# A 1024x6400 input projection: seven block products instead of eight for 34 of 50 column tiles on half of the tokens

## The chip, the cores and the metric

The kernel runs on one core of a Trainium2 chip. The core has a matrix engine (TensorE, PE in the profile, with its weight loads as PEld), a vector engine (VectorE, DVE), an engine for functions (ScalarE, ACT), a general one (GpSimd, POOL) and SyncE (SP), whose queue issues most of the DMAs here. The engines run at the same time and wait for each other by semaphores; each takes its own instructions strictly in the order of the program. The metric is the device time in microseconds, lower is better.

## What is computed

One layer of a decoder: a wide projection of 2080 tokens (2048 of a prompt, 32 of a sample group), three branches that mix tokens, a gate for each, an output projection and a layer norm.

```python
proj = x @ p['w_in']                      # (2080 x 1024) @ (1024 x 6400)
q, k, v, g_a, u_b, g_b, x_c, g_c, g_m = jnp.split(proj, _split_points(), axis=-1)
attn = _attn_prompt(q, k, v, ...)         # sliding window of 128, 8 heads
y_b = _s5_branch(u_b, ...)                # complex state-space scan, then a GLU
y_c = _rglru_branch(x_c, ...)             # convolution of 4, gated linear recurrence
ya = (attn * silu(g_a)) @ p['w_br_a']     # yb, yc in the same way from y_b, g_b and y_c, g_c
merged = sigmoid(g_m)[a] * ya + sigmoid(g_m)[b] * yb + sigmoid(g_m)[c] * yc
y = layernorm(DN_ALPHA * x + merged @ p['w_out'])
```

## The kernel before

Everything is float32. A product of two float32 matrices is made as three matmuls (`mm3`, L98 to L101): each operand is split into a high part (ACT, line L89) and the rest (DVE, L94 or L96), and high x high, high x rest and rest x high are added up in PSUM.

**Main line.** The 6400 columns of `w_in` are 50 tiles of 128 columns (`TILES`, 0 to 49, in the order u, x, k, v, q: 14 tiles; m: 24 tiles; gc, gb, ga: 4 each). The tokens are 5 units (`UN`): units 0, 1 and 2 of 512 tokens, units 3 and 4 of 272. Units 0 and 1 are called the first 1024 tokens here, units 2 to 4 the later ones. X, transposed and split, stays in SBUF (`xh0` to `xh4`, `xl0` to `xl4`). For a tile and a unit, `gemm` runs 8 blocks of the contraction x 3 matmuls into one of three PSUM banks (tag `mm`), and `evac` takes it out: a q, k, v, x or m tile by one ACT instruction and a store; a gate tile (gc, gb, ga) by ACT (tanh), DVE (L104, tanh+1 times the value) and DVE (L233, or L225 for gb, times the branch's result, loaded by `gate_load`), and a store of the product (`actD`). The weights of the next tile are split once in a tile (`w_split`, 128x1024 on ACT and DVE) and those after it are loaded (`w_load`).

**Side streams.** Four generators do the branches one after the other: `s5_stream`, `glu_stream`, `lru_stream`, `attn_stream`. The order on every engine is written out by hand: after each block of `gemm`, `tick(n)` adds 3n/2400 us to a counter, and when this has reached the value that the stream yielded last (`STEP` 4.6 where it gave none; 2.5 and 3.5 in turn for attention), the stream's next piece is emitted, its matmuls between those of the main line. So the side work of a microsecond of projection is fixed by these values, not by how far the engines are. The attention has 32 full steps (two for each of 16 blocks of 128 tokens). The gate tiles need the branch's result: gc that of the LRU (`hD`), gb that of the GLU (`zD`), ga that of the attention (`aD`).

**After the projection** come the branch projections (`y_unit`, tag `py`), where the last ga tile overlaps with the loads and splits of their operands (`seam`), and the output projection with the layer norm (`out_mm`, `out_ln`).

## Time and profile before

| | us |
|---|---|
| time, median of 3 runs | 1802.98 (1802.05 to 1808.93) |
| the profiled execution's own time | 1802.31 |
| its span, first to last instruction | 1800.6 |

The profile lists, for each engine, when its instructions began and ended. Matmuls are pipelined: one is listed longer than the time until the next begins, so the distance of starts is what one costs, and a share of busy time of PE near 100% tells little. For DVE, ACT and POOL a busy time is a real occupation of the engine. A line number is that of the kernel before; a helper (L89, L94, L96, L104) stands for many places, which the tile names tell apart. Side work and main line lie in the same stretches, so each stage is read by its own window.

### The profile page before, as it was taken

How to read it: one execution, taken by the hardware profiler on the slowest of the kernel's cores; microseconds unless marked ns; L12 is line 12 of the kernel's file. 1: busy time of each engine (PE TensorE's matmuls, PEld its weight loads, DVE VectorE, ACT ScalarE, POOL GpSimd, SP SyncE). 2: the span in 40 equal slices, each digit the busy share in tenths (PEclk: the TensorE clock that was granted, in tenths of full speed). 3: DMA queues.
4: the chain of work that ended last, by engine and by line, in shares of the span. 5: the costliest groups of instructions: out<-in, count | busy, mean ns of one | idle time of the engine just before them, and what ended most of it. 6: DMA issues, size and time to landing. Idle time of an engine off the chain costs nothing. (4 is left out here: it accounts for less than half of the span.)

```text
span 1800.6 us, 26639 instructions
## 1 busy us (share of the span) xinstructions
PE 1777.6 (99%) x9788; PEld 1548.2 (86%) x9788; DVE 1130.1 (63%) x2450; ACT 654.4 (36%) x1382; POOL 167.9 (9%) x377
## 2 busy tenths in 40 slices
PE   8999999999999999999999999999999999999998
PEld 7888888888899888888988888888888888888886
DVE  5755888885334455653777899644343657666666
ACT  6312443343333377674656555311221212120110
POOL 0000000000000000000355555400000000000000
PEclk9999999999999999999999999999999999999999
DMA  7443433442333334443332344453454646542222
GB/s 234 111 135 100 114 105 110 116 115 87 119 118 114 101 99 117 113 98 90 108 108 80 119 123 127 126 148 106 145 180 147 190 141 197 163 133 94 94 94 76
DMA packets 214039, 220.36 MB, mean 122 GB/s; under 512 B 89125, under 2 KB 156709, under 8 KB 212741
## 3 DMA queue, kind: packets, MB, share of 16 engines
q1 hardware_dynamic: 182532, 169.27, 33.3%
q10 hardware_dynamic: 31376, 49.39, 7.6%
q8 instruction: 77, 1.26, 0.3%
q14 instruction: 54, 0.43, 0.1%
HBM read 136.53 MB, written 83.14 MB: 122 GB/s over the span
## 5 line engine op out<-in xcount | busy, mean ns | idle before, releaser
L99 PE MATMUL mm<-xh,wh 128*128 128x512 f32 (+1 forms) x1920 | 678.3, 353 | 0.0
L101 PE MATMUL mm<-xh,wl 128*128 128x512 f32 (+1 forms) x1920 | 672.9, 350 | 0.0
L100 PE MATMUL mm<-xl,wh 128*128 128x512 f32 (+1 forms) x1920 | 670.8, 349 | 0.0
L101 PEld LDWEIGHTS mm<-xh,wl 128*128 128x128 f32 x1920 | 360.8, 188 | 47.2 <-DVE wl L94 0.3
L99 PEld LDWEIGHTS mm<-xh,wh 128*128 128x128 f32 x1920 | 361.3, 188 | 43.6
L100 PEld LDWEIGHTS mm<-xl,wh 128*128 128x128 f32 x1920 | 361.5, 188 | 42.7
L99 PE MATMUL py<-ah,wbh 128*128 128x512 f32 (+1 forms) x480 | 169.0, 352 | 1.3 <-DVE acc L104 1.3
L101 PE MATMUL py<-ah,wbl 128*128 128x512 f32 (+1 forms) x480 | 168.9, 352 | 0.0
L100 PE MATMUL py<-ah,wbh 128*128 128x512 f32 (+1 forms) x480 | 168.8, 352 | 0.0
L89 ACT ACTIVATE st<-mm 128x512 f32<-128x512 f32 (+1 forms) x170 | 86.8, 511 | 157.0 <-PE mm L101 144.9
L99 PEld LDWEIGHTS py<-ah,wbh 128*128 128x128 f32 x480 | 90.2, 188 | 14.5 <-issue 1.7
L100 PEld LDWEIGHTS py<-ah,wbh 128*128 128x128 f32 x480 | 90.3, 188 | 12.8
L101 PEld LDWEIGHTS py<-ah,wbl 128*128 128x128 f32 x480 | 90.2, 188 | 12.5
L1492 PE MATMUL po<-wol,mh 128*128 128x512 f32 x224 | 88.8, 396 | 0.0
L1491 PE MATMUL po<-woh,mh 128*128 128x512 f32 x224 | 88.8, 396 | 0.0
L1493 PE MATMUL po<-woh,ml 128*128 128x512 f32 x224 | 88.8, 396 | 0.0
L94 DVE TENSOR_TENSOR wl<-wr,wh 128x1024 fp32r<-128x1024 f32 x48 | 58.9, 1227 | 38.4 <-ACT wh L89 38.3
L104 DVE SCALAR_TENSOR_TENSOR gt<-gt,mm 128x512 f32<-128x512 f32 (+1 forms) x60 | 35.0, 583 | 70.8 <-ACT gt L89 70.5
L104 DVE SCALAR_TENSOR_TENSOR br<-br,py 128x512 f32<-128x512 f32 (+1 forms) x80 | 46.8, 586 | 51.5 <-PE py L101 43.8
L89 ACT ACTIVATE gt<-mm 128x512 f32<-128x512 f32 (+1 forms) x60 | 30.9, 515 | 115.6 <-PE mm L101 115.6
L89 ACT ACTIVATE wbh<-wbr 128x512 fp32r<-128x512 f32 x24 | 15.1, 629 | 149.1 <-PE py L100 127.6
L89 ACT ACTIVATE wh<-wr 128x1024 fp32r<-128x1024 f32 x48 | 50.5, 1052 | 24.6 <-DMA wr<-in_w_in_dram 15.3
(347 smaller groups left out, 2736.5 us busy)
## 6 DMA issues: line engine op xcount, KB each, us to landing
wr<-in_w_in_dram SPq DMA_DIRECT2D x48, 512.0 KB
mD<-st ACTq DMA_DIRECT2D x72, 256.0 KB
br<-mD SPq DMA_DIRECT2D x71, 256.0 KB
lx<-in_xr_dram SPq DMA_DIRECT2D x16, 512.0 KB
mD<-st ACTq DMA_DIRECT2D x48, 136.0 KB
br<-mD SPq DMA_DIRECT2D x47, 136.0 KB
xr<-in_xT_dram SPq DMA_DIRECT2D x24, 256.0 KB
wbr<-in_w_br_dram SPq DMA_DIRECT2D x24, 256.0 KB
```

What stands on the lines that cost most here:

```text
L89: return A.activation(out, in_, func, bias=bias, scale=scale, **kw)
L94: V.tensor_sub(lo, src, hi)
L99: PE.matmul(ps, wh, xh, start=start, stop=False)
L100: PE.matmul(ps, wh, xl, start=False, stop=False)
L101: PE.matmul(ps, wl, xh, start=False, stop=stop)
L104: return (eng or V).scalar_tensor_tensor(out, a, s, b, op0=op0, op1=op1)
L1491: PE.matmul(ps[c], h[:, k, :rows], wh, start=k == 0, stop=False)
L1492: PE.matmul(ps[c], h[:, k, :rows], wl, start=False, stop=False)
L1493: PE.matmul(ps[c], l[:, k, :rows], wh, start=False, stop=k == 7)
```

## The change

The order of the tiles is new: 14 tiles as before on all tokens (`FULL`), then the other 36 on the later tokens only (`LATER`: ga, gb, m, gc), then two gc tiles (48, 49) on the first 1024 tokens (`fill`), and then tiles 14 to 47 on the first 1024 tokens, in 17 pairs: two gc, four gb, 22 m, four ga and two more m tiles.

A pair is a product of a 2x2 block matrix of weights (two tiles x two halves of the contraction) with a 2x2 block matrix of X (two halves of the contraction x units 0 and 1). It is computed by seven block products of 4 blocks x 3 matmuls x 512 columns in place of eight. For that, sums of X blocks are made once (`x_sums` on DVE and POOL from a fresh load of X into the room of units 3 and 4, `x_parts` splits them), and for each pair sums of weight blocks (four POOL instructions in `operand`), seven splits of 128x512, four copies out of PSUM on ACT (`keep`) and four additions with PSUM on DVE. The weights of tiles 14 to 47 are loaded a second time (`pair_load`).

The gates: a later-token gate of ga or gb is stored without its branch (`gD`), and a new stream behind the attention, `gating_stream`, loads it and the branch and multiplies on POOL. gc on the later tokens and in `fill` is gated at once as before. In a pair, `finish` gates ga, gb and gc by two DVE instructions and one on ACT.

The GLU yields 2.8 in place of 4.6 in 16 places; the transposes of v go to the PSUM bank `sc`; `act_split`, `wo_split` and `m_split` use other rooms of the same pools (`xh1` is in two halves now). The core of the diff:

```diff
...
-GLU_WEIGHTS = 2.0
+GLU_WEIGHTS, GLU = 2.0, 2.8
...
          + [("q", i) for i in range(4)]
-         + [("m", i) for i in range(24)]
-         + [("gc", i) for i in range(4)] + [("gb", i) for i in range(4)] + [("ga", i) for i in range(4)])
+         + [("gc", 0), ("gc", 1)] + [("gb", i) for i in range(4)]
+         + [("m", i) for i in range(16, 24)] + [("m", i) for i in range(8, 16)] + [("m", i) for i in range(6)]
+         + [("ga", i) for i in range(4)] + [("m", 6), ("m", 7), ("gc", 2), ("gc", 3)])
+
+
+FULL, WIN = 14, 48
+
+LATER = sorted(range(FULL, len(TILES)), key=lambda i: ("ga", "gb", "m", "gc").index(TILES[i][0]))
 IN_NAMES = ["xT", "xr", "w_in", "w_br", "w_out", "w_glu", "lru_w", "lru_v", "lru0", "conv0",
             "s5p", "s5b", "s5c", "s5cd", "s5h", "s5hx", "s5d", "relT", "sinks", "ckT", "ck", "cv", "lnp"]
...
+        elif kind == "gc":
+            br = gate_br.pop((i, u))
+            st = stage.tile([128, 512], FT, name=uid("st"), tag="st")[:, :n]
+            act(st, ps[:, :n], AF.Tanh, scale=0.5)
+            V.tensor_mul(br, ps[:, :n], br)
+            stt(st, st, 1.0, br, OP.add, OP.mult)
+            gate_st.append((actD["c"][i][:, t0:t0 + n], st))
         else:
...
+            act(st, ps[:, :n], AF.Tanh, scale=0.5)
+            stt(st, st, 1.0, ps[:, :n], OP.add, OP.mult)
+            gate_st.append((gD[kind[1]][i][:, t0:t0 + n], st))
...
-            yield
+            yield GLU
...
-            ps = psum.tile([128, 512], FT, name=uid("mm"), tag="mm", bufs=3)
+            ps = sc()
...
+    def gating_stream():
...
+        for j, (b, i) in enumerate(jobs):
+            z, g = got.pop(j)
+            if b == "b":
+                gv = g[:, 0:1024].rearrange("p (c j) -> p c j", j=8)
+                G.tensor_mul(gv, gv, z[:, :, 0:128].rearrange("p j c -> p c j"))
+                gv = g[:, 1024:1056].rearrange("p (b t) -> p b t", t=4)
+                G.tensor_mul(gv, gv, z[:, 0:4, 128:136].rearrange("p t b -> p b t"))
+            else:
+                G.tensor_mul(g, g, z)
+            LD.dma_start(actD[b][i][:, 1024:T], g)
+            load(j + 2)
+            yield
+        es.close()
...
+    units = ([(o, u) for o in range(2, len(TILES)) for u in (range(5) if o < FULL else range(2, 5))][:-3]
+             + [(len(TILES) - 1, u) for u in (3, 4, 2)])
+    fill = [(WIN, 0), (WIN, 1), (WIN + 1, 1), (WIN + 1, 0)]
+    gated = [(ORDER[o], u) for o, u in units if TILES[ORDER[o]][0] == "gc"] + fill
...
+            sides += [glu_stream(), lru_stream(), attn_stream(), gating_stream()]
...
+        if (i, u) == gated[0]:
             while not gp:
                 side_step()
...
+    r12, r11, r22, r21 = (place(x, FT) for x in ("xl3", "xh3", "xh4", "xl4"))
+    for k in range(4):
+        for r, k0, c0 in ((r12, 0, 512), (r11, 0, 0), (r22, 4, 512), (r21, 4, 0)):
+            LD.dma_start(r[:, k], I["xT"][(k0 + k) * 128:(k0 + k) * 128 + 128, c0:c0 + 512])
+
+    def x_sums(k):
+        V.tensor_sub(r11[:, k], r12[:, k], r11[:, k])
+        G.tensor_sub(r12[:, k], r22[:, k], r12[:, k])
+        V.tensor_sub(r22[:, k], r22[:, k], r11[:, k])
+        G.tensor_sub(r21[:, k], r21[:, k], r22[:, k])
...
+    for n, (i, u) in enumerate(fill):
+        gates_out()
+        gate_next((i, u))
+        ps = gemm(i, u)
+        evac(*TILES[i], u, ps)
+        tick(512)
+        if n == 1:
+            for k in range(4):
+                x_sums(k)
+        if n > 1:
+            t = place(("xl2", "xh2")[n - 2])
+            TT[4 - n] = x_parts(t[:, 0:4], t[:, 4:8], (r22, r11)[n - 2])
...
+    def pair_load(i):
...
+            for j in range(2):
+                WD.dma_start(r[:, j], I["w_in"][i + j])
...
+    def operand(q):
...
+        a11, a12, a21, a22 = r[:, 0, 0:4], r[:, 0, 4:8], r[:, 1, 0:4], r[:, 1, 4:8]
+        if j == 0:
+            s1 = wpool.tile([128, 4, 128], FT, name=uid("s1"), tag="wr", bufs=1)
+            OPS["s1"] = s1
+            G.tensor_add(s1, a21, a22)
+        src = (a11, a12, a11, OPS["s1"], a21, a12, a22)[j]
+        w = wpool.tile([128, 2, 4, 128], FR, name=uid("ws"), tag=("wh", "wl")[q % 2])
+        split(w[:, 0], w[:, 1], src)
+        if j == 0:
+            G.tensor_sub(a21, a11, a21)
+            G.tensor_sub(a11, OPS["s1"], a11)
+        if j == 1:
+            G.tensor_sub(a12, a12, a11)
...
+    def keep(ps):
+        s = spare()
+        act(s, ps, AF.Copy)
+        return s
...
+    def finish(i, u, s):
+        kind, ti = TILES[i]
+        t0, n = UN[u]
+        if kind == "m":
+            act(s, s, AF.Tanh, scale=0.5)
+            ST.dma_start(mD[ti][:, t0:t0 + n], s)
+        else:
+            z = ZS.pop((i, u))
+            v = s.rearrange("p (c j) -> p c j", j=8) if kind == "gb" else s
+            V.tensor_mul(z, v, z)
+            act(s, s, AF.Tanh, scale=0.5)
+            stt(v, v, 1.0, z, OP.add, OP.mult)
+            gate_st.append((actD[kind[1]][ti][:, t0:t0 + n], s))
...
+    AHEAD = 3
+    pair_load(FULL)
+    for q in range(AHEAD):
+        operand(q)
+    TT[3] = x_parts(place("xh3"), place("xh4"), r12)
+    TT[4] = x_parts(place("xl3"), place("xl1a"), r21)
+    pair_load(FULL + 2)
+    blk = lambda u, k0: tuple([t[k0 + k] for k in range(4)] for t in X[u])
+    parts = lambda x: tuple([t[:, k] for k in range(4)] for t in TT[x])
+    MOV = [blk(0, 0), blk(0, 4), parts(2), parts(1), parts(3), blk(1, 4), parts(4)]
+    for p in range(FULL, WIN, 2):
+        if p == WIN - 4:
+            while sides:
...
+        while TILES[p][0] == "ga" and not prompt_done[0]:
+            side_step()
+        bank, kept = {}, {}
+        for j in range(7):
+            q = (p - FULL) // 2 * 7 + j
+            w, (mh, ml) = OPS.pop(q), MOV[j]
+            into, first = ((0, True), (1, True), (0, False), (2, True), (0, False), (2, False), (3, True))[j]
+            if first:
+                bank[into] = psum.tile([128, 512], FT, name=uid("mm"), tag="mm", bufs=3)
+            ps = bank[into]
+            for k in range(4):
+                for n, (a, b) in enumerate(((w[:, 0, k], mh[k]), (w[:, 0, k], ml[k]), (w[:, 1, k], mh[k]))):
+                    PE.matmul(ps, a, b, start=first and k == 0 and n == 0, stop=k == 3 and n == 2, skip_group_check=True)
+                if k < 3:
+                    tick(512)
+            operand(q + AHEAD)
+            gates_out()
+            if j == 0 and TILES[p][0] != "m":
+                z_load(p, 0)
+                z_load(p + 1, 1)
+            if j == 3:
+                pair_load(p + 4)
+            if j == 0:
+                kept[1] = keep(ps)
+            elif j == 1:
+                V.tensor_add(kept[1], ps, kept[1])
+                finish(p, 0, kept[1])
+            elif j == 2:
+                kept[2] = keep(ps)
+            elif j == 3:
+                kept[5] = keep(ps)
+            elif j == 4:
+                V.tensor_add(kept[5], ps, kept[5])
+                kept[3] = keep(ps)
+                finish(p + 1, 1, kept[5])
+            elif j == 5:
+                V.tensor_add(kept[2], ps, kept[2])
+                finish(p, 1, kept[2])
+            else:
+                V.tensor_add(kept[3], ps, kept[3])
+                finish(p + 1, 0, kept[3])
+            seam(p, j)
+            tick(512)
...
+        if t % 4 < 2:
+            if t % 4 == 0:
+                M_["mg"] = xhp.tile([128, 2, 2, 8, 128], FR, name=uid("mg"), tag="xh2")
...
+            m = xhp.tile([128, 2, 8, 128], FR, name=uid("mo"), tag=f"xh{t % 4 + 1}")
+            h, l = m[:, 0], m[:, 1]
...
```

## Rows read from the trace of the kernel before

**Rows 1.** The page, part 1: busy time, share of the span and count by engine.
```profile
PE 1777.6 (99%) x9788; PEld 1548.2 (86%) x9788; DVE 1130.1 (63%) x2450; ACT 654.4 (36%) x1382; POOL 167.9 (9%) x377
```

**Rows 2.** Timeline of PE: start, us, engine, line, tiles, shape.
```profile
1289.64 0.39 PE L99 MATMUL mm<-xh,wh 128*128 128x512 f32 x1
...
1299.16 0.28 PE L99 MATMUL mm<-xh,wh 128*128 128x272 f32 x1
...
1303.95 0.29 PE L101 MATMUL mm<-xh,wl 128*128 128x272 f32 x1
```

**Rows 3.** Windows: stretch, its us, busy (count) PE, PEld, DVE, ACT, POOL, clock, DMA.
```profile
853.00:1150.00 297.00, 290.69 (x1764) 258.65 (x1765) 246.44 (x535) 171.86 (x535) 154.53 (x300) 1.00 0.36 110
1050.00:1100.00 50.00, 47.66 (x296) 42.34 (x295) 46.34 (x99) 26.64 (x89) 26.44 (x51) 1.00 0.44 134
300.00:400.00 100.00, 100.00 (x574) 88.67 (x573) 83.94 (x230) 41.79 (x88) 1.18 (x12) 1.00 0.39 107
```

**Rows 4.** Timeline of DVE: the first and the last scores of the attention, a gate.
```profile
854.79 0.29 DVE L1038 TENSOR_TENSOR S<-sa,B 128x128 f32<-128x128 f32 x1
...
1140.20 1.44 DVE L225 TENSOR_TENSOR st<-gt,br 128x512 f32<-128x512 f32 x1
1141.57 0.94 DVE L1040 TENSOR_TENSOR S<-sa,B 128x768 f32<-128x768 f32 x1
```

**Rows 5.** Groups of DVE in 853:1150: line, tiles, shape, count | busy, mean ns.
```profile
L94 DVE TENSOR_TENSOR wl<-wr,wh 128x1024 fp32r<-128x1024 f32 x10 | 12.4, 1244 | 2.9 <-ACT wh L89 2.9
L104 DVE SCALAR_TENSOR_TENSOR gt<-gt,mm 128x512 f32<-128x512 f32 x14 | 9.5, 680 | 0.6 <-ACT gt L89 0.5
L233 DVE TENSOR_TENSOR st<-gt,br 128x512 f32<-128x512 f32 x12 | 9.3, 777 | 0.4
L233 DVE TENSOR_TENSOR st<-gt,br 128x272 f32<-128x272 f32 x8 | 3.6, 447 | 0.3
L104 DVE SCALAR_TENSOR_TENSOR gt<-gt,mm 128x272 f32<-128x272 f32 x8 | 3.4, 428 | 0.1
L225 DVE TENSOR_TENSOR st<-gt,br 128x512 f32<-128x512 f32 x2 | 2.5, 1238 | 0.1
```

**Rows 6.** Groups of PE, whole span: the attention's matmuls.
```profile
L1026 PE MATMUL sa<-kl,q 128*128 128x192 f32 x120 | 28.4, 274 | 0.0
L1052 PE MATMUL sc<-ident,S 128*128 128x128 f32 x128 | 19.8, 278 | 3.5 <-DVE S L1012 2.7 <-ACT oo L89 0.7
L1100 PE MATMUL sb<-pth,vn 128*128 128x256 f32 x62 | 18.1, 292 | 0.7 <-POOL pth L1082 0.7
```

**Rows 7.** Groups of DVE, whole span: a split and an addition with PSUM.
```profile
L94 DVE TENSOR_TENSOR wbl<-wbr,wbh 128x512 fp32r<-128x512 f32 x24 | 16.4, 684 | 0.0
L1059 DVE TENSOR_TENSOR ptl<-sc,pth 128x512 fp32r<-128x512 f32 x32 | 21.9, 683 | 0.9 <-ACT pth L89 0.5
```

**Rows 8.** Groups of ACT, whole span: a copy out of PSUM, a split.
```profile
L89 ACT ACTIVATE st<-mm 128x512 f32<-128x512 f32 x102 | 60.2, 590 | 104.7 <-PE mm L101 102.9 <-DMA ur<-uD 1.1 <-ACT st L89 0.4
L89 ACT ACTIVATE wbh<-wbr 128x512 fp32r<-128x512 f32 x24 | 15.1, 629 | 149.1 <-PE py L100 127.6 <-DMA wbr<-in_w_br_dram 12.3 <-DVE acc L1459 9.2
```

**Rows 9.** Groups of POOL, whole span: the longest of either kind.
```profile
L1082 POOL TENSOR_SCALAR_AFFINE_SELECT pth<-pth 64x256 fp32r<-64x256 f32 x60 | 32.5, 561 | 2.0
L991 POOL CAST vn<-vn 64x512 fp32r<-64x512 f32 x16 | 12.9, 806 | 56.3 <-DVE vn L94 55.5
```

**Rows 10.** Timelines of DVE and POOL: the same DVE instruction without and beside POOL.
```profile
867.03 0.42 DVE L978 TENSOR_TENSOR kl<-kr,k 64x256 fp32r<-64x256 f32 x1
...
902.80 0.49 POOL L1082 TENSOR_SCALAR_AFFINE_SELECT ptq<-pth 64x256 fp32r<-64x256 f32 x1
...
903.05 0.51 DVE L978 TENSOR_TENSOR kl<-kr,k 64x256 fp32r<-64x256 f32 x1
```

**Rows 11.** Timelines of PE, ACT and DVE: end of one GLU product to the next.
```profile
522.12 0.40 PE L99 MATMUL mm<-xh,wh 128*128 128x512 f32 x1
...
522.32 0.61 ACT L89 ACTIVATE zs<-sb 128x528 f32<-128x528 f32 x1 [2.59 <-PE sb L101]
...
525.99 1.26 DVE L96 SCALAR_TENSOR_TENSOR zl<-zy,zh 128x1056 fp32r<-128x1056 f32 x1 [1.15 <-ACT zh L89]
...
527.59 0.28 PE L99 MATMUL sa<-zh,gluh 128*128 128x264 f32 x1
```

**Rows 12.** The page, part 2: what the DMA engines moved, 40 slices.
```profile
GB/s 234 111 135 100 114 105 110 116 115 87 119 118 114 101 99 117 113 98 90 108 108 80 119 123 127 126 148 106 145 180 147 190 141 197 163 133 94 94 94 76
```

279 lines of the change are left out of this document (163 added, 116 removed).

## The prediction

> **What bounds the kernel now.** I read the page by engine first, then the distance of matmul starts, then each stage by its window. PE is busy for 99% of the span [rows 1], which alone proves little; but the distances do: in an undisturbed unit 42 starts of 512 columns lie (1299.16 - 1289.64) / 42 = 0.2267 us apart and 38 of 272 columns (1303.95 - 1299.16) / 38 = 0.126 us [rows 2]. That is columns + 32 at 2.4 GHz, the higher clock level, in both; I use it for shapes that I don't show. A column tile then costs 24 x (3 x 0.2267 + 2 x 0.126) = 22.4 us on all tokens, and the projection's 50 tiles 1119 us of the 1800.6. So PE's matmuls are the path, and a matmul taken away is worth 0.2267 us, as long as no other engine becomes the path. The second thing to read is therefore DVE by stage: 63% over the span, but 246.4 of 297 us while the attention runs, and 46.34 of 50 where gates and attention meet; there PE is busy for 47.66 of 50 only [rows 1, 3].
>
> **What is removed.** A pair of tiles takes 7 x 4 x 3 = 84 matmuls of 512 columns instead of 96. 17 pairs x 12 x 0.2267 = 46.2 us of PE, on the path. All other matmuls stay, in number and size. The profiled execution took 1802.31 us, 0.7 under the median of 1802.98, so the sum is made against 1802.3: with nothing else, 1756.
>
> **The attention beside the pairs.** Its pieces are tied to the projection's columns, so I count them in the program. A step of the attention takes 2.5 + 3.5 of the counter; with 512 columns a block that is 4 + 6 blocks, 10 x 3 x 0.2267 = 6.8 us of projection (7.2 in the smaller units; 6.9 over the old stretch). The same count, made for the old order, puts the end of the attention into the first gb tiles; the trace has the gate of gb (L225) just ahead of the last scores [rows 4], so the count holds. From first to last scores are 31 steps in 286.8 us [rows 4], 9.25 us each: 6.9 of projection and, by counts of [rows 6], 8 x 0.093 + 4 x 0.067 + 6 x 0.12 = 1.7 of its own matmuls, with the transposes of v 1.8. The rest, 0.5 us a step or 16 us in 32 steps, PE waits already now.
>
> DVE in this stretch: 246.4 us less splits and gates, 12.4 + 9.5 + 9.3 + 3.6 + 3.4 + 2.5 = 40.7 [rows 3, 5], leaves 206 for 32 steps, 6.4 each.
>
> In the new order the count puts the first step into the second gc tile on later tokens. There follow 2.7 such tiles, the four units of `fill`, and nine pairs: gc, two gb, six m. PE needs 2.7 x 24 x (0.2267 + 2 x 0.126) = 31 us, 4 x 5.44 = 22, 9.1 x 84 x 0.2267 = 173, and 32 x 1.8 = 58: 284 us. DVE needs, from [rows 5, 7]:
> - attention: 206;
> - 2.7 later gc tiles: 1.24 + 0.68 + 0.78 + 2 x (0.43 + 0.45) = 4.5 each: 12;
> - `fill` and the sums of X: 8 sums and 16 splits at 0.68, 4 gates at 1.46: 22;
> - nine pairs: 7 splits + 4 additions = 11 x 0.68 = 7.5 each: 67;
> - their gates: gc 4 x 1.46 = 6; two gb pairs, both instructions on strided data like L225, 4 x 2 x 1.24 = 10 each: 20.
>
> That is 333 us of DVE against 284 of PE: in this stretch DVE becomes the path. The additions out of PSUM don't wait long either: a bank that held the copy's source (`keep`) is written again one product, 12 x 0.2267 = 2.7 us, later, and ACT and DVE take attention and pairs in one queue, where a unit before had two further banks. Were DVE busy all the time, the stretch is 333 us; at the share of the fullest window, 46.34 / 50 = 0.93 [rows 3], 358. I take the middle, 345. So PE waits 61 us where it waited 16: **+45, between +33 and +58**. ACT stays under it: 172 us now [rows 3], and a pair brings 7 x 0.63 + 8 x 0.59 = 9.1 us [rows 8], nine of them 82.
>
> **The S5 stage.** DVE is at 84% there [rows 3]. Its last 81 us of projection (by the count) now lie beside ga and gb tiles on later tokens, with a split and a gate every 11.5 us: 1.24 + 0.68 + 2 x 0.43 = 2.8 us, where it was a split in 22.4. That is 24% instead of 6% of DVE, 15 us more in a stretch of some 92: just full. +3, between 0 and 8.
>
> **The GLU's 2.8.** Between two products of the GLU PE now does 5.47 us of projection (522.12 to 527.59), while ACT and DVE make the next operand: from the end of the product to the end of zl at 527.25 are 5.1 us [rows 11]. With 2.8 it is 5 blocks, 15 x 0.2267 = 3.4 us. The second half of each of the 8 products feeds the next, so 7 times 5.1 - 3.4 = 1.7: +12, between 0 (if the first half's chain ends earlier for it) and 14.
>
> **Hidden.** Loading X again, 16 x 256 KB, takes 4.2 MB / 234 GB/s = 18 us [rows 12] behind 16 us of matmuls; the first pair's weights, 1 MB or 4.5 us, are queued on SP behind a gate's store, that behind the sums. I take nothing for both, since DVE's list above ends later; up to +10 if not, and what then stands is the first block product. Weights loaded again, 17.8 MB: a pair moves 1 MB in and 1 MB out in 19 us, 110 GB/s beside the attention, below the 190 that a slice reached [rows 12]. POOL's sums (68 + 8) have no like here: 64x256 took 0.56 and 64x512 0.81 us [rows 9], so 0.8 to 1.1 us for 128x512, at most 4.5 us a pair beside 154.5 / 32 = 4.8 a step: 18 of 26 us. The later gates move to POOL behind the attention, where it is idle; their stores hold SP while POOL multiplies, and pair loads with them, which are 19 us early. The order of `seam`, the banks of `vtr` and the rooms of `m_split` change no count: 0, up to +3 for the bank shared with the transposes.
>
> The Trainium skill (GPSIMD Engine Reference, 3.1) has a two-input operation on POOL at about twice DVE's time; by that a sum would be an estimated 1.4 us, POOL at 19 of 26 us a pair, and the total the same.
>
> **Sum.** 1802.3 - 46.2 + 45 + 3 + 12 = 1816 us.
>
> **Rivals.** (1) DVE's list is fitted in: PE waits no more than now, the GLU's chain included. 1756 to 1768; with half of the waits, 1793. For it: at 93% of DVE PE lost only 2.3 of 50 us [rows 3]. Against it: the list is 117% of PE's. Chance 0.35, of which 0.28 under 1794. (2) The shared port, slower: an instruction of DVE with two operands in SBUF beside one of POOL took 0.51 us where it took 0.42 alone [rows 10]. The pairs put 36 more POOL instructions beside a DVE that is full, and `fill` 8. If each held DVE for its own 0.8 to 1.1 us, 35 to 48 us come on top: 1851 to 1864; half of it 1838. It decides from the point where DVE has no idle time left, in the gate pairs and `fill`. Chance 0.15. The Trainium skill (SBUF — State Buffer, Who interferes with whom) states this as a full block for the whole instruction; by that rule the upper end holds, while the 0.09 us of the row speak for a part of it. (3) The attention hasn't begun when gc needs `hD`: LRU pieces are emitted bare, two or three at some 9 us, 1838. The count leaves one tile, 11 us, of room. Chance 0.05.
>
> **How the numbers follow.** The forecast case, 1800 to 1838, has 0.45, a third of it under 1812. What a measurement can tell from no change is about 0.5%, 1794 to 1812. Faster 0.28 (rival 1); same 0.07 of rival 1 + 0.15 + 0.02 of rival 3 = 0.24; slower 0.30 + 0.15 + 0.03 = 0.48. The range of 8 in 10 leaves out the lower third of rival 1 and the upper half of rival 2: 1768 to 1850.
>
> **What would show it.** In the new profile: 204 matmuls fewer; the pairs' matmuls at 0.2267 us where PE doesn't wait; DVE above 90% from the gc tiles to the ninth pair, and PE's gaps there in front of products whose split or addition is late; the gb pairs longest, some 36 us with their steps, an m pair some 26, a pair behind the attention 19; GLU products 1.7 us late. Wrong would be a DVE under 85% in this stretch with PE unbroken (then 1), or POOL ahead of DVE's waits (then 2).

## The result and the profile after

The changed kernel took 2003.76 us (median of four runs, 2000.12 to 2011.22) beside 1802.51 us for the kernel before on the same chip: a ratio of 1.1119, 95% interval 1.1091 to 1.1147. The forecast was 1816 us with a range of 1768 to 1850. The direction was the likeliest of the three named, the size is out of the range by 154 us. The profiled execution's span is 1998.4 us, 197.8 more than before.

The page of the kernel after, part 1 (busy time, share of the span and count by engine) and two lines of part 2 (40 slices of the span):

```profile
PE 1806.3 (90%) x9584; PEld 1553.2 (78%) x9584; DVE 1291.1 (65%) x2633; ACT 764.7 (38%) x1585; POOL 305.0 (15%) x465
...
DVE  5856888973445655467788867765455366767766
...
PEclk9999999999999999989788888899979999999999
```

Against [rows 1]: 204 matmuls fewer, as counted; DVE 161 us more, POOL 137 us more. DVE is at 65% over the span, and in the slices from 900 to 1300 us, where the attention lies, between 60 and 89%; the shares alone name no bound. What is new is the last line: the granted clock is down from 850 to 1300 us, and once more at 1450.

To say where the time went I took the distance of each matmul's start from the next and split it in three: *needed* is (columns + 32) / 2.4 GHz, the pitch of [rows 2]; *lower clock* is what a distance has beyond that where it fits the lower level of 1.2 GHz; the rest is *wait*. The split goes by distances alone and takes in some short waits (before, the granted clock is 0.998 over the span, so hardly any of its 13 us can be the clock's); it is read by differences. PE's waits that are given below without a row are sums of this split. Over the span before: 1734.8 needed, 13.1 lower clock, 38.8 wait. After: 1688.5, 71.3 and 225.3. So the needed time fell by 46.3 us, and 58 us of lower clock and 187 us of waits came. By stage:

```
stage of the kernel after                us           lower clock + wait   the same work before
S5 with u, x, k, v, q                    0:400        13.8                 9.9
GLU beside later tokens                  400:640      24.7   }             3.5
LRU beside later tokens                  640:881      37.4   }
attention, first to last score           881:1315    169.4                18.0
rest of the pairs, gating, branches      1315:1998    51.3                20.4
```

The windows of the kernel after, columns as in [rows 3]:

```profile
400.00:640.00 240.00, 225.05 (x1436) 205.74 (x1437) 121.92 (x223) 89.27 (x140) 0.40 (x4) 0.97 0.37 114
640.00:881.00 241.00, 217.44 (x1262) 192.89 (x1261) 126.55 (x160) 149.76 (x220) 0.81 (x4) 0.94 0.44 117
881.00:1315.00 434.00, 323.13 (x1558) 266.99 (x1557) 336.73 (x635) 219.22 (x618) 217.03 (x334) 0.85 0.31 98
...
1400.00:1640.00 240.00, 216.44 (x1002) 179.39 (x1001) 119.50 (x177) 69.66 (x127) 46.83 (x28) 0.94 0.61 192
```

The third line is the case. The forecast's list for DVE in this stretch was 333 us; it did 336.73. But it took 434 us for them, 78%, where the forecast let it go at 93 to 100%, by the fullest 50 us of before; over the whole stretch that answers to it [rows 3] it had been at 83%, behind a PE that hardly stood. What PE needs there is 263.8 us.

The chain of work that ended last, from 1099.97 us (start, us, engine, tile, line), shows how DVE and ACT pass the work on while PE waits:

```profile
1099.97 1.42 DVE st L111
1101.39 0.88 DVE S L1049
...
1105.51 0.96 DVE q L111 x2
...
1109.47 0.61 DVE br L1635
...
1110.10 1.77 DVE gt L1576
...
1112.62 1.55 ACT S L96 x8
1114.19 0.17 DVE m L1019
...
1114.60 0.15 DVE S L1021
```

For twelve microseconds DVE has work without a gap: a gate of a gb pair (strided, 1.42), the scores' front, the low parts of q and k, an addition of the pair, the gate's product (1.77). ACT's tanh of the pair overwrites an operand of that last product, so it waits for it; the exponentials of the attention stand behind that tanh on ACT; the softmax's last step on DVE stands behind the exponentials; and PE's transposes of S wait for that. PE, DVE and ACT in the stretch, by what they waited for (us in total, times, longest):

```profile
PE sc L1061 <- DVE S L1021: 37.6, 11, 8.3
PE sc L993 <- DVE ptl L1068: 30.1, 8, 15.6
PE mm L1611 <- ACT st L96: 15.6, 4, 6.1
...
DVE m L1019 <- ACT S L96: 30.4, 16, 3.3
DVE ws L101 <- ACT ws L96: 17.5, 20, 4.6
DVE T L1484 <- POOL T L1483: 8.5, 4, 2.4
...
ACT br L96 <- DVE st L1631: 34.1, 8, 7.6
ACT br L96 <- DVE gt L1576: 25.1, 6, 7.4
```

DVE's 97 us of idle time are hand-overs: to 88 us the profile gives a name, and in 73 of these it is an instruction of ACT. ACT in its turn waits there for DVE: 116 us for the additions and the gates' products of the pairs (L1576, L1624, L1631, L1635, L1638), of which two rows are shown.

Groups of DVE and POOL in the stretch (columns as in [rows 5]):

```profile
L101 DVE TENSOR_TENSOR ws<-T,ws 128x512 fp32r<-128x512 f32 x52 | 43.9, 846 | 15.7 <-ACT ws L96 15.1
...
L1068 DVE TENSOR_TENSOR ptl<-sc,pth 128x512 fp32r<-128x512 f32 x30 | 20.4, 681 | 0.4
```

```profile
L1528 POOL TENSOR_TENSOR s<-T 128x512 f32<-128x512 f32 x9 | 13.4, 1484 | 6.3 <-DMA T<-in_w_in_dram 6.1
L1536 POOL TENSOR_TENSOR T<-T 128x512 f32<-128x512 f32 x9 | 12.5, 1388 | 9.4 <-DVE ws L101 9.1
```

The split of a weight operand has the shape of [rows 7] and takes 0.846 us instead of 0.684, while `ptl`, from PSUM, still takes 0.681. POOL's sums take 1.39 to 1.48 us; the forecast's estimate, 0.8 to 1.1, was from instructions with one operand [rows 9].

### The profile page after: what moved, and what is told of

Its sections match the earlier page's. It is cut to its first block, busy times and chain, and to the rows that moved or that the text cites. A ratio compares the mean times of both kernels' runs of the same rounds, so it can differ in the third digit from the quotient of the medians.

```text
span 1998.4 us, 27020 instructions
## 1 busy us (share of the span) xinstructions
PE 1806.3 (90%) x9584; PEld 1553.2 (78%) x9584; DVE 1291.1 (65%) x2633; ACT 764.7 (38%) x1585; POOL 305.0 (15%) x465
## 4 chain that ended last, share of the span: by engine, by line
PE 60%; DVE 18%; ACT 9%; DMA 6%; issue 5%; POOL 2%; ACTq 1%; SPq 1%; DVEq 0%; POOLq 0%
PE mm L108 9%; PE mm L106 8%; PE mm L107 8%; PE mm L1611 6%; PE py L106 4%; PE py L108 4%; PE py L107 4%; PE po L1717 3%; PE po L1718 3%; PE po L1716 3%; DMA wr<-in_w_in_dram 2%; DVE ws L101 1%; ACT st L96 1%; DVE q L111 1%; DVE xf L111 1%
## 5 line engine op out<-in xcount | busy, mean ns | idle before, releaser
L106 PE MATMUL mm<-xh,wh 128*128 128x272 f32 (+1 forms) x1264 | 424.4, 336 | 16.1 <-DVE st L111 8.2
L108 PE MATMUL mm<-xh,wl 128*128 128x272 f32 (+1 forms) x1264 | 423.4, 335 | 13.2 <-DVE wl L101 13.1
L107 PE MATMUL mm<-xl,wh 128*128 128x272 f32 (+1 forms) x1264 | 420.4, 333 | 0.0
L108 PEld LDWEIGHTS mm<-xh,wl 128*128 128x128 f32 x1264 | 241.0, 191 | 37.8 <-DVE wl L101 16.7
L106 PEld LDWEIGHTS mm<-xh,wh 128*128 128x128 f32 x1264 | 241.9, 191 | 36.6 <-DVE st L111 8.7
L1611 PE MATMUL mm<-T,ws 128*128 128x512 f32 x816 | 225.5, 433 | 44.5 <-ACT st L96 29.5
L107 PEld LDWEIGHTS mm<-xl,wh 128*128 128x128 f32 x1264 | 241.9, 191 | 20.0
L1611 PEld LDWEIGHTS mm<-T,ws 128*128 128x128 f32 x816 | 168.3, 211 | 87.5 <-ACT st L96 33.8
L101 DVE TENSOR_TENSOR ws<-T,ws 128x512 fp32r<-128x512 f32 x102 | 88.5, 870 | 55.2 <-ACT ws L96 54.6
L1611 PE MATMUL mm<-xh,ws 128*128 128x512 f32 x272 | 96.9, 424 | 10.2 <-ACT ws L96 10.2
L96 ACT ACTIVATE wh<-wr 128x1024 fp32r<-128x1024 f32 x48 | 50.6, 1054 | 79.6 <-DMA wr<-in_w_in_dram 66.2
```

Source lines behind the costliest of these rows:

```text
L96: return A.activation(out, in_, func, bias=bias, scale=scale, **kw)
L101: V.tensor_sub(lo, src, hi)
L106: PE.matmul(ps, wh, xh, start=start, stop=False)
L107: PE.matmul(ps, wh, xl, start=False, stop=False)
L108: PE.matmul(ps, wl, xh, start=False, stop=stop)
L1611: PE.matmul(ps, a, b, start=first and k == 0 and n == 0, stop=k == 3 and n == 2, skip_group_check=True)
```

## The experiments

Four theories are told apart. **A**: DVE's list of work is too long for the stretch. **B**: POOL's two-operand sums hold DVE. **C**: queues: an instruction that waits holds what stands behind it on its engine, and a block product leaves its PSUM bank only one product, 2.7 us, of slack. **D**, formed later: the attention's own chain through DVE and ACT. The cuts of the edits are against the kernel after; "..." stands for lines left out.

The attention's steps make a common measure. From the first score of one step to that of the next, mean of the 31 distances, with DVE's busy and idle time in it; *excess* is the period less what PE needs in it (8.51 us; with the longer pace of e7 and e18 11.14; in e5 2.63 on the mean, since 26 of its steps have no projection beside them, 1.76).

```
kernel                  time us (ratio, 95% interval)     period   DVE busy  idle   excess
before                  1802.5                             9.21     7.64     1.57    0.60
after                   2003.8 (1.112, 1.109 to 1.115)    13.97    10.86     3.11    5.46
e1 no weight sums       1975.5 (1.095, 1.092 to 1.098)    13.24    10.16     3.08    4.73
e2 finish later         1973.3 (1.094, 1.091 to 1.097)    13.36    10.92     2.44    4.85
e3 v in another bank    2000.5 (1.109, 1.103 to 1.115)    13.92    10.90     3.02    5.40
e4 later weights        1999.0 (1.108, 1.105 to 1.111)    13.96    10.86     3.11    5.45
e5 attention first      2030.7 (1.127, 1.124 to 1.131)     7.81     7.02     0.79    5.18
e6 plain products       1914.9 (1.063, 1.058 to 1.068)    10.80     8.36     2.44    2.29
e7 attention's pace     2042.4 (1.134, 1.131 to 1.137)    16.36    11.99     4.37    5.22
e8 high parts           1970.6 (1.094, 1.090 to 1.098)    13.08     9.59     3.49    4.58
e9 low parts apart      2009.6 (1.116, 1.113 to 1.119)    14.00    10.79     3.21    5.47
e10 tanh apart          1994.7 (1.107, 1.103 to 1.112)    13.69    10.87     2.82    5.18
e11 first pair          1997.7 (1.109, 1.106 to 1.112)    13.82    11.12     2.70    5.31
e12 e2,e3,e9,e10,e11    1967.7 (1.092, 1.089 to 1.096)    13.00    11.13     1.87    4.47
e13 bank slack          2012.2 (1.116, 1.112 to 1.120)    14.29    10.99     3.30    5.79
e14 e13,e2,e11          1989.7 (1.104, 1.099 to 1.108)    13.69    11.13     2.56    5.18
e15 plain, two banks    1918.6 (1.064, 1.060 to 1.068)    10.91     8.40     2.51    2.40
e16 own bank            1989.4 (1.104, 1.100 to 1.107)    13.77    10.91     2.86    5.27
e17 e16,e2,e10,e11      1959.8 (1.087, 1.083 to 1.092)    12.97    11.15     1.82    4.47
e18 e16,e7              2005.2 (1.112, 1.109 to 1.116)    15.41    11.99     3.42    4.27
```

### The order of the tiles or the block products: e6 and e5

**e6**, the order kept, the block products undone:

```diff
-        for j in range(7):
...
-            operand(q + AHEAD)
...
-                V.tensor_add(kept[3], ps, kept[3])
-                finish(p + 1, 0, kept[3])
+        for j, (i, u) in enumerate(((p, 0), (p + 1, 0), (p, 1), (p + 1, 1))):
+            ps = gemm(i, u)
...
+            finish(i, u, keep(ps))
```

> One part undone: the order of the tiles, the stored gates, the gating stream and the copies out of PSUM stay, but each pair is made by four plain products of 24 matmuls, 96 instead of 84 to a pair; X is not loaded again, and there are no sums of X, of weights or of products. Theory A: DVE's list falls by 7 x 0.68 less two splits of 1.24 and by 4 additions to a pair, some 5 us of 7.5, so DVE stays under PE: the time is that of before plus the GLU's 12, 1810 to 1825. Theory B (POOL's two-operand sums hold DVE): the same, 1810 to 1825, since POOL's sums are gone. Theory C: a product lasts 5.4 us instead of 2.7, so a late operand or bank is forgiven twice as much; the waits of 895 to 1300 us (128 in the changed kernel) fall to 40 to 60, while the late weights of the later tiles (27) and the gating stores on SP (30) stay: 46 more matmul time, 1860 to 1900.

1914.88 us: 112 us above before, 89 below after, a little above C's range, 90 us above that of A and B. The new order and what goes with it (the stored gates, the gating, the copies out of PSUM, the GLU's 2.8) cost more than half of the loss without any block product. Lower clock and waits by the stages of the table above: 13.8, 24.4, 35.0, 71.0 and 16.6. So the GLU's and the LRU's stage lose the same as in the kernel after, the attention's 71.0 (53 more than before), the rest nothing. The seven products then save 46.3 needed and cost 98 in the attention's stretch (169.4 - 71.0) and 35 behind it (51.3 - 16.6). Its window of the attention:

```profile
879.00:1214.00 335.00, 295.54 (x1555) 248.82 (x1554) 259.14 (x533) 191.38 (x549) 159.51 (x290) 0.95 0.35 110
```

DVE has 259 us of work here and PE needs 264: neither is over the other, and still 71 us are lost. That alone is not a list that is too long (A).

**e5**, the attention in one piece ahead of `fill`:

```diff
+    while not prompt_done[0]:
+        side_step()
     TT = {}
     for n, (i, u) in enumerate(fill):
```

> One part undone: the attention no longer runs beside the pairs. What is left of it when the later tokens' tiles are done is emitted in one piece ahead of `fill`, and the pairs follow with the gating alone. Theory A (DVE's list is too long for the stretch, the prediction's): bare steps cost DVE's 6.4 us each, some 26 of them 170 us, and the pairs then run at 19.0 us; the stretch of fill, attention and first nine pairs comes to 22 + 170 + 173 = 365 us where the changed kernel takes 405 in 895 to 1300: total 1955 to 1980. Theory C (queues: one instruction that waits holds what stands behind it on ACT, DVE or SP, and a pair has one product of slack): pairs behind the attention lose almost nothing but what the gating stores cost on SP; a bare step is a chain through ACT, DVE and PE and takes 9 to 12 us, 26 of them 235 to 310 us: total 2020 to 2090. In both, the first nine pairs alone at 19 to 20 us say that the waits of 895 to 1300 us belong to the sharing and not to the pairs themselves; pairs at 22 or more would say that the pairs carry them alone.

2030.69 us, C's lower end. Its windows, bare attention and pairs alone:

```profile
930.00:1114.00 184.00, 110.68 (x444) 91.16 (x444) 165.60 (x360) 105.91 (x360) 114.31 (x240) 0.56 0.18 51
1400.00:1500.00 100.00, 100.00 (x443) 82.84 (x442) 45.17 (x60) 44.77 (x79) 30.28 (x22) 1.00 0.32 111
```

From 1338 to 1529 us ten pairs run at 19.0 us each without a wait: m and ga pairs by themselves are what the forecast took them for. The six before them (gc, two gb, three m, the gating beside the later ones) took 19.2 to 34.9 us, 160 us for 114, with PE waiting mostly for ACT to empty a bank (21 us). So the expectation's "19 to 20" does not hold for the first nine, and a part of the pairs' loss needs no attention beside them. A bare step takes 7.7 us, of which DVE works 90%. That is neither A's 6.4 (7.0 of work a step, and it doesn't run at 100% even here) nor C's 9 to 12. The bare attention follows DVE, and PE stands in it: the granted clock is 0.56 there, near the lower level.

### How long the list is, and POOL: e8, e7, e1

**e8**, 119 subtractions left out:

```diff
-        split(w[:, 0], w[:, 1], src)
+        act(w[:, 0], src, AF.Copy)
...
```

> One cost taken out: the low parts of the 119 weight operands are left out (the subtractions on DVE, 0.87 us each in the changed kernel, 103 us in all, some 60 of it beside the attention); the same number of matmuls runs, with the high part in place of the low, so that the output is that of rounded weights. Theory A: DVE's list goes from 333 to 270 us, under PE's 284, and the excess is gone: total 1920 to 1945. Theory B: POOL's sums still hold DVE, but a DVE with room: 1950 to 1970. Theory C: the subtractions run three products ahead of their use, and PE doesn't wait for them; what they hold is the queue for a few steps: 1970 to 1995.

1970.59 us, on the border between B's range and C's. DVE's list in the stretch fell by 39 us (1.27 a step), the period by 0.89: the rest turned into idle time of DVE (3.49 from 3.11). A's 60 to 80 us are out, but work taken off DVE is worth most of itself, which C had not said.

**e7**, more projection beside each step:

```diff
-ATT_SCORE, ATT_SOFTMAX = 2.5, 3.5
+ATT_SCORE, ATT_SOFTMAX = 3.3, 4.6
```

> One size changed: the attention's two pieces are emitted every 3.3 and 4.6 us of projection instead of 2.5 and 3.5, so that its 32 steps lie beside twelve pairs instead of nine. Theory A: DVE's list has some 70 us more of PE beside it, so that its excess of 49 us is gone: waits and lower clock of the stretch fall by 60 to 80, total 1920 to 1945. Theory C: each step brings its waits along wherever it lies; a little more distance helps a little, and the end runs into the gating: total 1975 to 2005.

2042.42 us, slower than either theory had it. 2.6 us more of PE's work lie beside a step, and its excess hardly moves: 5.22. The time that is lost goes with the number of steps, not with how much of PE's time they are spread over; a later end of the attention then costs some 72 us of waits from 1430 to 1535 us, around the ga pairs, whose gate needs it, 41.4 of them in one piece. In place of the transposes PE now waits for the pairs' additions:

```profile
PE mm L1611 <- DVE br L1635: 51.8, 12, 5.4
```

Each of the twelve is an addition that stands on DVE behind the low parts of q and k. DVE's work a step grew by 1.13 us, since more of the pairs' work lies beside a step too. This fells A in its simple form.

**e1**, POOL's sums of weights left out:

```diff
...
-            G.tensor_add(s1, a21, a22)
+            OPS["s1"] = a22
...
-            G.tensor_sub(a21, a11, a21)
-            G.tensor_sub(a11, OPS["s1"], a11)
...
-            G.tensor_sub(a12, a12, a11)
```

> The kernel after with the four POOL sums of each pair's weights left out (68 instructions of 1.41 us, 96 us of POOL): the seven products take the raw weight blocks, so what is computed is not the projection; all matmuls, splits and additions stay. Three theories for the 200 us: A, throughput: DVE's list is longer than PE's in the attention stretch; B, the port: POOL's two-operand sums hold DVE's two-operand instructions (a split took 0.87 us in place of 0.68, 1.6 at worst); C, the queues: an instruction that waits on one engine holds what stands behind it on ACT, DVE or SP, PE has one product of slack, and its clock falls after each wait. A: the list hardly changes, 1995 to 2004 us. B: the blocked time goes and with it the waits behind it, 1940 to 1965. C: only what waits for the sums themselves, 1980 to 1995.

1975.45 us: 28 less, between B and C. DVE's instructions take 0.70 us less a step, 22 us over 31 steps, with none of them removed; its idle time stays. So B is real and its price is some 25 us of the 201. A place where it is seen, the timelines of DVE and POOL of the kernel after, columns as in [rows 10]:

```profile
1215.77 0.51 DVE L987 TENSOR_TENSOR kl<-kr,k 64x256 fp32r<-64x256 f32 x1
1216.31 2.16 DVE L111 SCALAR_TENSOR_TENSOR q<-qr,q 64x256 fp32r<-64x256 f32 x2
1218.50 1.39 DVE L987 TENSOR_TENSOR kl<-kr,k 64x256 fp32r<-64x256 f32 x1
1219.92 1.64 DVE L101 TENSOR_TENSOR ws<-T,ws 128x512 fp32r<-128x512 f32 x1
...
1218.18 1.43 POOL L1528 TENSOR_TENSOR s<-T 128x512 f32<-128x512 f32 x1
1219.68 1.33 POOL L1533 TENSOR_TENSOR T<-T 128x512 f32<-128x512 f32 x1
```

`kl`, 0.42 alone and 0.51 beside a one-operand instruction [rows 10], takes 1.39 beside a sum of 1.43. All thirty of these in the kernel after go that way: two alone at 0.42, 25 beside one-operand instructions at 0.51 to 0.53, three beside sums at 1.39 to 1.40.

### Moving single instructions: e2, e3, e4, e9, e10, e11, e12

Each of these leaves the work as it is and moves one thing that the waits point at.

**e2**, a product is finished one product later:

```diff
+            while pend:
+                finish(*pend.pop(0))
...
-                finish(p, 0, kept[1])
+                pend.append((p, 0, kept[1]))
...
```

> The kernel after with each finish (tanh or gate, and store) emitted one product later, so that ACT doesn't stand at the tanh of a sum that DVE hasn't reached; no work is added or removed. A and B: the lists and the port are as before, 1998 to 2010 us. C: ACT reaches the copies out of PSUM and the attention's exponentials earlier, 30 to 60 us less, 1945 to 1975.

1973.3 us, as C had it; DVE's idle time goes from 3.11 to 2.44 a step, its busy time stays.

**e3**, the transposes of v in the second bank of `sb`:

```diff
-            ps = sc()
+            ps = pv_[0][:, 1] if pv_ else sc()
             PE.transpose(ps[:, 0:128], QK[b][2], ident)
...
```

> The kernel after with the transposes of v in the unused second bank of the attention's output tile instead of the bank sc. In the trace of after PE stood 31 us in front of these transposes (L993), 16 us of it once. A and B: another wait takes the place, 1995 to 2008 us. C: most of the 31 us goes, and some of the low clock behind, 1965 to 1980.

2000.47 us; C's 25 us didn't come. PE's waits in front of these transposes fell from 31 to 26 us, and those in front of the products with v rose from 9 to 19 us.

**e4**, the later tiles' weights asked for from ACT's queue:

```diff
-            WD.dma_start(WR[i], I["w_in"][i])
+            (WD if o <= FULL + 1 else ST).dma_start(WR[i], I["w_in"][i])
```

> The kernel after with the weight loads of the later-token tiles issued from ACT's queue instead of SP's, where the stores of the LRU wait for DVE. In the trace of after ACT stood 66 us for these loads and PE 27 us for the weights, between 465 and 900 us, ahead of the pairs. A and B explain nothing there: 1998 to 2008 us. C: 25 to 40 us less, 1963 to 1978, with PE unbroken between 640 and 880 us but for the GLU.

1999.0 us, as A and B had it. The reason was right and the remedy wrong. SP's queue in 640:881, of the kernel after:

```profile
SPq L926 <- DVE hs L925: 63.2, 4, 18.8
```

and of the kernel before, in the stretch of its LRU:

```profile
SPq L917 <- DVE hs L916: 73.6, 4, 19.3
```

SP stands just as long for the LRU's stores in both kernels. But a tile was 22.4 us long before and is 11.5 us long on the later tokens, so that a load that is 16 us late is hidden there and not here; ACT's splits then wait for it 66.2 us over the span (15.3 before), a group of the kernel after:

```profile
L96 ACT ACTIVATE wh<-wr 128x1024 fp32r<-128x1024 f32 x48 | 50.6, 1054 | 79.6 <-DMA wr<-in_w_in_dram 66.2
```

On ACT's queue the loads are on time (ACT waits 4 us for them from 640 to 900 us), but PE gains little: between 465 and 900 us the waits in front of the projection's matmuls go from 25 to 15 us in the profile's rows, those in front of the LRU's own from 3 to 14. The loss of 640:881 falls from 37.4 to 29.7 us.

**e9**, the low parts of q and k moved behind the softmax, in two halves:

```diff
-            if n < 32 and kv == 1 and b + 1 < 16:
-                low()
...
+                elif b + 1 < 16:
+                    low(0)
+                    yield 1.6
+                    low(1)
...
```

> One order changed: the low parts of q and k for the next block (six instructions on DVE, 3.6 us and more, emitted in one go behind the scores in every second step of the attention) move behind the softmax, in two halves 1.6 us of projection apart. Count, pace and length of all instructions stay. What is to be told apart: does the fixed wait of 4.3 us a step (4.2 also with 11.3 us of projection to a step in place of 8.5) come from bursts in DVE's queue, behind which a pair's addition and with it ACT's next tanh and the exponentials stand? If so (theory C, as bursts), the wait falls to 2 to 3 us a step: 45 to 70 us with the clock, total 1930 to 1955. Theory A (list) and B (POOL): no instruction less, 1990 to 2005.

2009.63 us: a miss, above both ranges. The waits in front of the transposes fell from 46 to 8 us, and in their place the scores wait for q: 58 us in front of L1034 and L1035. The burst is shifted, not covered.

**e10**, the tanh in a buffer of its own:

```diff
+            h = spare()
+            act(h, s, AF.Tanh, scale=0.5)
             V.tensor_mul(z, v, z)
-            act(s, s, AF.Tanh, scale=0.5)
...
```

> One wait taken away: the tanh of a gate tile goes to a buffer of its own and stands ahead of DVE's product with z, so that ACT no longer waits until DVE has read the operand that the tanh overwrites. It concerns the three gate pairs beside the attention and the two beside the gating. Theory C: ACT's rows of 42 and 35 us behind that product shrink, and with them the exponentials and PE's transposes of S in the gate pairs; PE's waits 30 to 50 us less: total 1945 to 1970, if the two buffers more in use don't hold PE in their turn. A and B: 1990 to 2005.

1994.73 us: 9 less where 30 to 50 were expected, and the two intervals still overlap. DVE's idle time 2.82.

**e11**, the start of the pairs:

```diff
-    def x_sums(k):
-        V.tensor_sub(r11[:, k], r12[:, k], r11[:, k])
...
+    def x_sums():
+        for e, o, a, b in ((V, r11, r12, r11), (G, r12, r22, r12), (V, r22, r22, r11), (G, r21, r21, r22)):
+            for k in range(4):
+                e.tensor_sub(o[:, k], a[:, k], b[:, k])
...
+        if n == 3:
+            pair_load(FULL)
```

> The start of the pairs alone: the first pair's weights are asked for one unit earlier, ahead of a gate's store in SP's queue, and the sixteen sums of X are emitted by operation and not by k, so that DVE doesn't wait for POOL at each k. Theory C: the two waits at 940 and 968 us (15.7 and 10.4 us) go down to a few us: total 1975 to 1985. A: the same work on DVE, 1995 to 2005.

1997.73 us: a miss as well. Of the two waits the first went from 15.7 to 13.4 us, the second stayed at 10.4. DVE no longer waits for POOL there, but its sums and splits, one after the other, still stand ahead of the attention's `ptl`.

**e12**, the five together:

> All changes of order and buffers together: a product finished one product later, the transposes of v in the second bank of sb, the low parts apart, the tanh apart, the start of the pairs. Under theory C waits give way once no in-order queue is left that joins the two streams closely: the stage from 895 to 1300 us keeps 2 us a step, total 1870 to 1910. Under A and B every one of these leaves the list as it is, and the sum can't go below what the finishing alone gave: 1960 to 1975.

1967.69 us, where A and B had it: 36 us under after, and the same as e2 alone within the intervals. DVE is busy for 86% of the stretch and its idle time is 1.87 a step; the period doesn't go under 13.0. That is as far as these moves of order came.

### The slack of a bank: e13 to e18

**e13**, a fourth bank and another order of the seven products:

```diff
+    JORD = (0, 3, 1, 2, 5, 6, 4)
+    SB.append(sb())
+    banks = [psum.tile([128, 512], FT, name=uid("mm"), tag="mm", bufs=3) for _ in range(3)] + [SB[0][:, 1]]
```

> One size changed: the pairs get a fourth bank (the second half of sb, which the attention leaves empty), and the seven products come in the order 1, 4, 2, 3, 6, 7, 5 of the old count, so that two to four other products, 5.4 us and more, lie between a product and the next one into its bank, instead of one (2.7 us). Matmuls, copies, additions and sums keep their number and length. Theory C, as slack: bursts of 5 us in DVE's or ACT's queue (which the moves of single instructions only shifted from one wait to another) are now covered for the products themselves; PE's rows of the pairs' matmuls fall to near nothing and the attention's waits with them, as its chain is no longer held behind a waiting copy: wait per step from 4.3 to 2 to 3 us, total 1925 to 1960. A rival (D): the wait is the attention's own chain through DVE and ACT, as long beside the pairs as bare; then the waits reappear in front of the transposes of S and the scores, 1985 to 2005.

2012.21 us, above both ranges. On the three old banks PE's waits between 1000 and 1280 us fell from 20 to 1 us, but the fourth is half of a tile that the attention uses, and products into it wait for the eviction of the other half:

```profile
PE sb L1612 <- DVE oo L1117: 39.6, 10, 12.2
```

**e16** keeps e13's order and gives the fourth bank a tile of its own:

```diff
+        pes.close()
+        p4.append(ph1.enter_context(tc.tile_pool(name="ps4", bufs=1, space=PSUM)))
...
+    banks = [psum.tile([128, 512], FT, name=uid("mm"), tag="mm", bufs=3) for _ in range(3)] + [p4[0].tile([128, 512], FT, name="m4", tag="m4", bufs=1)]
...
```

> The fourth bank again, now as a tile of its own: sb is given back when the attention begins, and its two banks become one for the attention's products with v and one for the pairs. In the run with the shared tile PE's waits for additions fell from 20 to 1 us on the three old banks, but products in the shared tile waited 37 us for the attention's eviction of the other half. Theory C, as slack: these 37 and 15 us go, the 20 stay away, and nothing comes in their place: 88 us of waits between 1000 and 1280 us become 45 to 60, total 1955 to 1980. Theory D (the attention's own chain): the transposes of S and the scores wait that much longer: 1990 to 2005.

1989.36 us, D's value. The waits for additions are gone from all banks (24 us to 2 over the stretch), and the attention's own have come in their place: scores for q and k 23 instead of 7, transposes of S and v 80 instead of 78. PE's waits in the stretch of the attention:

```profile
PE sc L999 <- DVE ptl L1074: 31.5, 7, 15.6
PE sc L1067 <- DVE S L1027: 26.5, 11, 7.5
PE sa L1040 <- DVE q L111: 15.0, 5, 5.6
```

The period is 13.77 instead of 13.97. So the banks' slack, a part of C, was not what held the steps: with it lifted PE mostly waits for the same DVE at another place, and 14 us are won.

**e15**, less slack for the plain products:

```diff
+            two.reverse()
+            ps = two[0]
-        ps = psum.tile([128, 512], FT, name=uid("mm"), tag="mm", bufs=3)
```

> The other way round: the kernel with four plain products to a pair, but with two banks for them instead of three, so that one product of 5.4 us lies between two into the same bank instead of two (10.9 us). Theory C, as slack: wait per step goes from 1.8 to about 2.5 to 3.5 us, total 1935 to 1965. Theory D: the same as with three banks, 1910 to 1922.

1918.6 us, the same as with three banks within the intervals: D again.

**e14**, e13 with e2 and e11, and **e17**, e16 with e2, e10 and e11:

> The fourth bank and the order of the run before, with the products finished one product later and the pairs' start put right (first weights asked for earlier, sums of X by operation). Theory C: the parts add up, since each takes away another reason for a queue to stand: 1890 to 1930. Theory D: what the finishing alone gave, 1965 to 1980.

> The bank of its own, with the products finished one product later, the tanh in its own buffer and the pairs' start put right. Theory C: the parts add up, since none waits for another's queue any more: 1910 to 1945. Theory D: 1960 to 1980, as with the finishing alone.

1989.66 us, 10 above D's range, and 1959.8 us, D's lower end. e17 is the fastest of the kernels with seven whole products, and 157 us slower than before. Its window and DVE's waits:

```profile
883.00:1286.00 403.00, 323.27 (x1558) 267.60 (x1557) 346.19 (x638) 220.00 (x619) 226.93 (x335) 0.87 0.34 108
```

```profile
DVE ws L101 <- ACT ws L96: 16.4, 17, 3.9
DVE m L1025 <- ACT S L96: 6.0, 7, 1.2
```

DVE's waits for the exponentials are down to 6 from 30 us; what is left is a DVE at 86% with 346 us of work in a stretch where PE needs 264.

**e18**, the bank of its own at the longer pace:

> The bank of its own and the longer pace of the attention (3.3 and 4.6) together. At the longer pace alone the wait a step stayed at 4.2 us, but most of it stood in front of the pairs' matmuls (41 and 14 of 72 us between 1000 and 1280 us), and little in front of the transposes of S; at the old pace it was the reverse (41 of 88 us in front of the transposes). Two limits, then: the time between scores and transposes at the old pace, the bank's slack at the new one. Theory C: with both lifted the wait a step falls under 2 us in the stretch; the total, which the attention's forced end in front of the ga pairs sets, 1975 to 2010. Theory D: 4 us a step stay, 2035 to 2050.

2005.16 us, in C's range by the total; but the excess a step is 4.27 and the wait 3.4 us, neither C's 2 nor D's unchanged 4. PE now waits for the pairs' operands (36 us) and for the transposes of v (26) between 1000 and 1361 us; again both are DVE's.

### What the runs together say

In the attention's stretch a step with pairs beside it takes what DVE works in it plus 1.8 to 4.4 us in which DVE waits, mostly for ACT. That DVE is the path there is true in the main: of the chain of work that ended last, 46% of the stretch is DVE's in the kernel after, 19% ACT's and 12% PE's; in e17 DVE has 54%, in e18, at the longer pace, 37% beside 27% of PE. Of the 5.46 us a step, 2.35 are DVE's work beyond what PE needs (10.86 - 8.51), and 0.70 of these are POOL's doing (e1); 3.11 are DVE's idle time, of which a better order gave back 1.3 (e17; the step became 1.0 shorter, since DVE's work in it grew by 0.3). C in its first form (short slack of the banks) fell with e16; what is left of it is that DVE and ACT hand work to each other in two in-order queues, and that fell by two fifths with the order. What sets the last 1.8 us of idle time isn't settled: in e8 a shorter list left more of it, and no run took the pairs' share of ACT away. Nor is it shown which part of the order makes a step of e6 1.6 us longer than before (0.7 of DVE's work, 0.9 of its idle time).

## Why the prediction was right or wrong

**What is removed.** Right: 204 matmuls, 46.3 us of needed time for 46.2.

**The attention beside the pairs.** The mechanism was right in half, and this is the term that was mis-sized: +45 (33 to 58) for a measured +151 (169.4 against 18.0). DVE's list is longer than PE's there, as forecast, but that makes 2.35 of the 5.46 us a step; the other 3.11 are idle time of DVE, and the sign that the forecast named, a DVE above 90%, did not come. The list was good to 1% (333 and 336.73 us), in part by luck: by e1 some 22 us of the measured work are what POOL's sums add, which the list didn't have. What lies beside which pair was right too: the ninth ends 15 us after the last score. The step that failed is the one from list to time. It took DVE's share between 93% and 100% from the fullest window [rows 3]; measured is 78%, 434 us instead of 345. In that window of before DVE's waits for ACT come to 1.8 us; in the stretch after they come to 73, since each of DVE's round trips through ACT counts where PE no longer sets the pace, and ACT itself stands for 116 us for the pairs' additions and gate products on DVE. The forecast named just that, ACT and DVE taking attention and pairs in one queue, and gave it no price. A share of 78% on 333 us would have given 427. A part of the loss is the price of PE's gaps: the clock was granted at 0.85 in the stretch, some 35 of the 169 us by the split above.

The pairs are longer than said: gc 46.5, gb 38.7 and 39.9, m beside the attention 33 to 45 us (said: gb 36, m 26); m behind it 20 to 27 us, while the last part of the attention and the gating ran, with one at 19.1 (said: 19).

**The S5 stage.** Right: +3, measured 13.8 - 9.9 = 3.9, nearly all of it one wait for DVE's gate of a unit, at 396 us.

**The GLU's 2.8.** Right in its term: PE waits 11.6 us in front of the fourteen matmuls of zh and zl, for 12. Timeline of the kernel after, the answer to [rows 11]:

```profile
504.35 0.39 PE L108 MATMUL mm<-xh,wl 128*128 128x512 f32 x1
...
504.89 0.39 PE L106 MATMUL sa<-zh,gluh 128*128 128x264 f32 x1 [0.16 <-ACT zh L96]
...
506.19 0.39 PE L107 MATMUL sa<-zl,gluh 128*128 128x264 f32 x1 [0.90 <-DVE zl L103]
```

Not priced: 4.7 us for a late load of the GLU's weights, at 466 us (ACT stands 10.5 us for it, with an eviction behind it), and some 7.5 us of lower clock. The granted clock is low three times in this stage: behind the wait at 396 us, behind that at 466, and once, at 566, behind one of the GLU's gaps.

**Hidden.** The step that was wrong besides the share. It weighed the pairs' weights and left out those of the later tiles, with +34 in the LRU's stage (37.4 against at most 3.5 for the whole stretch before): half as long a tile behind the same SP (e4). The start of the pairs cost 15.7 and 10.4 us of waits, for "up to +10". The later gates and their stores on SP, taken at 0 because pair loads are 19 us early, lie in the stage that lost 31 us more than before behind the attention. Wait rows of 1400 to 1640 us:

```profile
SPq L1516 <- DVE ws L101: 23.4, 3, 22.2
...
ACT st L96 <- DVE gt L1576: 18.6, 2, 9.9
ACT br L96 <- DVE gt L1576: 17.1, 4, 9.0
```

A pair load stood 22.2 us on SP until a split had read its buffer, and the gate operands behind it came late. With the same gating e6 loses 16.6 us behind the attention, no more than before, where 51.3 are lost here: it is the gating together with the pairs of seven products that costs, and how the 31 us divide between them is not shown. POOL's sums: 1.36 to 1.47 us over the span for an estimate of 0.8 to 1.1. The Trainium skill (GPSIMD Engine Reference, 3.1) has a two-input addition on POOL at about twice DVE's time; the estimated 1.4 us that followed from it agree with the trace.

**The sum.** -46.3 + 3.9 + 58.6 (GLU and LRU, of which 12 were priced) + 151.4 + 30.9 = 198.5 us, for 197.8 of span.

**The rivals.** (1), the list fitted in, fell: 169 us. (2), the shared port, holds as a mechanism: e1 gives 28 us for the sums of the weights alone, where 35 to 48 stood for all sums if each held DVE for its own time. The Trainium skill (SBUF — State Buffer, Who interferes with whom) has a DVE instruction with two inputs in SBUF contend with a POOL instruction that reads SBUF, and calls the contention an exclusive lock. The 1.39 us of `kl` beside a sum of 1.43 agree with that; the 0.09 us of [rows 10], beside a POOL instruction with one operand, are less than a lock would cost. (3), the attention not begun, didn't come about: of the 37 us lost in the LRU's stage 4.3 stand in front of its own matmuls.

**The range.** One end of DVE's term was a DVE that is never idle, the other a share from a kernel in which DVE was not the path; with the share taken as unknown, a range that lets it fall to 0.75 (a value picked with the result known) has 444 us for the list and a total near 1915, still 89 under the measured time: most of the rest is what the stages outside the attention lost. Nor had it a price for the lower clock, 58 us over the span.

## What to carry to other kernels

An engine's share in a stretch where it follows another doesn't tell the share that it reaches when it becomes the path itself: here 93% promised and 78% came, with a list that was counted right; bare, without any second stream, it was 90%. Count for every stage the time from a load's issue to its use against the length of the unit that hides it, also where the change only makes that unit shorter. And if moving single instructions shifts a wait from one matmul to another of the same engine's making, look at that engine's whole round, busy and idle, before moving the next.
